# Prompt and sample tokens transposed once, unnormalized; their norm applied behind and between the value projections, in a written order

## The chip, the cores and the metric

The kernel runs on one core of a Trainium2 chip. The metric is the device time of one execution in microseconds (us). A NeuronCore has engines that run side by side, each through its own instructions in order: PE (TensorE, matmuls and transposes; PEld is its loading of weights), DVE (VectorE), ACT (ScalarE), POOL (GpSimd) and SP (SyncE, which here issues most DMAs). They meet through semaphores. Matmuls accumulate in PSUM and DVE or ACT empty it.

## The reference

One step of a two-layer decoder over 1104 tokens: 64 sample tokens (8 requests of 8), 16 meta tokens and 1024 prompt tokens. What the change touches is the beginning of the first layer, an mLSTM mixer on normalized tokens:

```python
def rmsnorm(x, g):
    xf = x.astype(jnp.float32)
    r = lax.rsqrt(jnp.mean(xf * xf, axis=-1, keepdims=True) + EPS)
    return (xf * r * g.astype(jnp.float32)).astype(x.dtype)

def mlstm_mixer(xn, C0, n0, m0, lead, w_in, b_ig, b_fg, mh_g, w_out):
    p = xn @ w_in
    ...
    q = heads(p[..., :HK], DK_A) * DK_A ** -0.5
    k = heads(p[..., HK:2 * HK], DK_A)
    v = heads(p[..., 2 * HK:2 * HK + HV], DV_A)
    og = p[..., 2 * HK + HV:2 * HK + 2 * HV]
    gi = p[..., 2 * HK + 2 * HV:2 * HK + 2 * HV + H_A]
    gf = p[..., 2 * HK + 2 * HV + H_A:]
    ...

def run_trunk(h, C0, n0, m0, lead, attend, prm):
    ...
            a, (C, n, m) = mlstm_mixer(rmsnorm(h, prm['norm_a'][i]), C0[i], n0[i], m0[i], lead, ...)
            h = h + a
```

Here HK is 512, HV is 1024 and the model width is 1024. A SwiGLU follows, then an attention layer on a paged cache with forget values, and a second SwiGLU. `r` is the root of the title (one number per token), `g` the gain (one number per feature).

## The kernel before

All is fp32. Each product is made of three matmuls of fp32r: an operand x is split into a high half xh (a cast, on ACT) and a low half xl = x - xh (on DVE), and `mm3` (lines 191 to 195) adds xh by high weights, xh by low weights and xl by high weights. Halves of weights are called whi and wlo, raw ones wraw.

The 1104 tokens are nine tiles: tile 0 with 80 tokens (samples and meta), tiles 1 to 8 with 128. The 1024 features are eight blocks of 128.

`load_x` (line 628) brings one tile after another into `xin` by DMA from SP, makes the sum of squares and the root on ACT (L644, L645), its reciprocal (L646) and the normalized `xn` on DVE (L647). It transposes `xn` on PE (tile xps, L655) and splits it into xh and xl (L267, L268), which stay in SBUF for all projections. It also transposes the raw `xin` (tile hps, L661), copies that into `hs` (L662, one half on DVE and one on ACT) and writes it to `hD` in DRAM (L663, DMA from POOL), the residual stream that the rest of the kernel reads back.

`phase_a` then makes the values in four groups of 256 columns, c in (3, 0, 1, 2) (line 92), through `tm_proj` (line 306): nine tiles each, 24 matmuls per tile into a PSUM tile `tmps`, of which there are four; `evac` copies them into `vA` on ACT (L695). Group 3 carries 16 gate columns more (L697). Next come `cache_prep` (line 807: 32 small DMAs of cached log-forget values through a page table, four transposes, a running sum on DVE, L829, eight DMAs to `csE`), three of the eight column blocks of `w_out_a` halved and written to DRAM (`wo_out`), and the q and k projections (`qk_out`, PSUM tile mmA). The gates are prepared next to them (`rec_prep`), then the gate projections and the recurrence follow.

Up to `qk_out` the order on each engine is set by the scheduler, from what is ready; PE's first rows below show how it mixes both transposes with group 3.

Of the kernel before, what the change touches and what calls it, by code (L numbers as in the profile page):

```python
# [93 lines left out]
class TwoNorms:  # L94
# [11 lines left out]
    def low(self, o, y, h):  # L106
        self.sub(o, y, h.bitcast(F32))
# [69 lines left out]
class Net:  # L177
# [19 lines left out]
    def consts(self):  # L197
# [15 lines left out]
        with self.pool("g0") as gp, self.pool("g0p", space=PSUM) as pp:  # L213
            rows = gp.tile([NG, P], F32, name="grows")
            for at, src, n in (
                (G_A, I["norm_a"][0], 8), (G_F, I["norm_ffn"].rearrange("l d -> (l d)"), 16),
                (G_KV, I["norm_kv"], 8), (G_B, I["norm_b"][0], 8), (G_FIN, I["norm_final"], 8),
                (G_MH, I["mh_norm_a"][0].rearrange("h d -> (h d)"), 8),
            ):
                nc.scalar.dma_start(rows[at : at + n, :], src.rearrange("(k p) -> k p", p=P))  # L220
            ps = pp.tile([P, NG], F32, name="gps")
            nc.tensor.transpose(ps, rows, self.ident[:NG, :NG])
            nc.vector.tensor_copy(self.gain, ps)
# [395 lines left out]
def _add(cls):  # L619
    def deco(f):  # L620
        setattr(cls, f.__name__, f)
        return f

    return deco


@_add(Net)
def load_x(self):

    nc, I = self.nc, self.I  # L630
    with self.pool("lx", bufs=2) as lp, self.pool("lxp", bufs=2, space=PSUM) as pp:
        gr = lp.tile([P, D], F32, name="gr", bufs=1)
        nc.scalar.dma_start(gr, I["norm_a"][0].partition_broadcast(P))
        for i, (t0, t1) in enumerate(TT):
            n = t1 - t0
            xin = lp.tile([P, D], F32, name="xin", bufs=3)
            if i == 0:
                nc.sync.dma_start(xin[:NS], I["x_sample"].rearrange("b t d -> (b t) d"))
                nc.sync.dma_start(xin[NS:T0], I["meta_tokens"])
            else:  # L640
                nc.sync.dma_start(xin, I["x_prompt"][0, (i - 1) * P : i * P, :])
            xn = lp.tile([P, D], F32, name="xn")
            r = lp.tile([P, 2], F32, name="r0")
            nc.scalar.activation(xn[:n], xin[:n], AF.Square, accum_out=r[:n, 0:1])  # L644
            nc.scalar.activation(r[:n, 1:2], r[:n, 0:1], AF.Sqrt, scale=1.0 / D, bias=self.eps[:n])  # L645
            nc.vector.reciprocal(r[:n, 1:2], r[:n, 1:2])  # L646
            nc.vector.scalar_tensor_tensor(out=xn[:n], in0=xin[:n], scalar=r[:n, 1:2], in1=gr[:n], op0=ALU.mult,  # L647
                                           op1=ALU.mult)
            hs = lp.tile([P, KT, P], F32, name="hs")
            for g in range(2):  # L650
                ks = slice(4 * g, 4 * g + 4)
                ps = pp.tile([P, 4, P], F32, name=self.uid("xps"), tag="xps")
                for k in range(4):
                    f = 4 * g + k
                    nc.tensor.transpose(ps[:, k, :n], xn[:n, f * P : (f + 1) * P], self.ident[:n, :n])  # L655
                xh, xl = self.xs
                self.split(ps[:, :, :n], xh[:, ks, t0:t1], xl[:, ks, t0:t1])
                ps = pp.tile([P, 4, P], F32, name=self.uid("hps"), tag="hps")
                for k in range(4):
                    f = 4 * g + k  # L660
                    nc.tensor.transpose(ps[:, k, :n], xin[:n, f * P : (f + 1) * P], self.ident[:n, :n])  # L661
                (nc.scalar.copy if g else nc.vector.tensor_copy)(hs[:, ks, :n], ps[:, :, :n])  # L662
            nc.gpsimd.dma_start(self.hD[:, :, t0:t1], hs[:, :, :n])  # L663


@_add(Net)
def phase_a(self, vt):
# [5 lines left out]
    with ExitStack() as c3:  # L673
# [14 lines left out]
        with ExitStack() as cw, self.pool("ppA0", bufs=4, space=PSUM) as pp:  # L688
            self.wpools(cw, 3, 4)
            self.load_x()  # L690
            for c in (3, 0, 1, 2):
                c0 = 2 * HA * DK + 256 * c

                def evac(i, m, ps):
                    nc.scalar.copy(v(i)[:m, 2 * c : 2 * c + 2, :DV], ps[:m, :256].rearrange("p (h d) -> p h d", h=2))  # L695
                    if c == 3:
                        nc.scalar.copy(gates[:m, i, :], ps[:m, 256:272])  # L697

                self.tm_proj([w_in[:, c0 : c0 + 256]] + ([w_in[:, 3072:3088]] if c == 3 else []), None, pp, "mm0", 4,
                             evac)  # L700
                if c == 3:
                    for n, out in ((NQ, self.q8), (NM, self.m16)):
                        self.row_mask(kp.tile([P, P // n, n], F32, name=self.uid("rm"), tag="rm"), out, n)

        pp = c3.enter_context(self.pool("ppA", bufs=2, space=PSUM))

        self.wpools(c3, 2, 3, side="left")
        self.cache_prep()


        self.woD = []

        def wo_out():
            m = len(self.woD)
            d = self.dram.tile([P, 2, KT, P], F32, name=f"woD{m}")
            for z, y in enumerate(self.load_w([I["w_out_a"][0][:, m * P : (m + 1) * P]])):
                nc.gpsimd.dma_start(d[:, z], y.bitcast(F32))
            self.woD.append(d)
# [88 lines left out]
def cache_prep(self):  # L807
# [5 lines left out]
    with self.pool("cp") as sp, self.pool("cpp", space=PSUM) as pp:  # L813
        lp = sp.tile([P, NPG, NB, HB], F32, name="lp")
        for b in range(NB):
            for n in range(NPG):
                j = b * NPG + n
                v = nc.sync.value_load(self.ptab[0:1, j : j + 1], min_val=0, max_val=I["cache_k"].shape[0] - 1)
                self.pages.append(v)
                nc.sync.dma_start(lp[:, n, b, :], I["cache_logf"][bass.DynSlice(v, 1)].rearrange("a p h -> (a p) h"))  # L820
        cs = sp.tile([P, PAST], F32, name="cs")
        lt = sp.tile([P, PAST], F32, name="csl")
        on = sp.tile([P, PAST], F32, name="cso")
        ps = pp.tile([P, 512], F32, name="csps")
        for n in range(NPG):
            nc.tensor.transpose(ps[:, n * P : n * P + P], lp[:, n].rearrange("p b h -> p (b h)"), self.ident)
        nc.scalar.activation(lt, ps, AF.Copy, scale=-1.0)
        nc.gpsimd.memset(on, 1.0)
        nc.vector.tensor_tensor_scan(cs, on, lt, 0.0, ALU.mult, ALU.add)  # L829
        nc.vector.tensor_copy(self.clast, cs[:, PAST - 1 : PAST])  # L830
        for q in range(NQ):
            nc.gpsimd.dma_start(self.csE.rearrange("b (h q) k -> q b h k", q=NQ)[q].rearrange("b h k -> (b h) k"), cs)
# [2012 lines left out]
```

## Time and profile before

| | |
|---|---|
| three runs, median (lowest to highest) | 2835.35 us (2833.57 to 2840.07) |
| the profiled execution | 2837.3 us |
| its span, first to last instruction | 2835.5 us, 60526 instructions |
| mean granted clock of PE | 0.996 |
| DMA | 469.45 MB, mean 166 GB/s |

The profile belongs to one execution, so times taken from it are set against 2837.3 us, not the median. Busy time of an engine is no bound by itself: a group of rows names the line, the engine, the operation, output and inputs by tile, how many, then busy us and mean ns, then the idle time before them and what ended it. Matmuls overlap in the array, so what a matmul costs is read from the distance of starts, not from its length.

### The profile page before, as it was taken

Reading aid. Unit: us, or ns where it says so; the run is one execution under the profiler, and the core shown is the slowest. Engines: PE = TensorE matmul, PEld = TensorE weight load, DVE = VectorE, ACT = ScalarE, POOL = GpSimd, SP = SyncE. Lnnn points to the kernel's source line nnn. Section 1 sums busy time; section 2 is a strip of 40 time slices with the busy share of each in tenths; the row PEclk is TensorE's granted clock in tenths of the full one; section 3 lists DMA queues with packets and bytes.
Section 4 is the critical chain, followed back from the end, with each engine's and each line's share of the span. In section 5 each row is a group of like instructions: output and inputs, shape, how many; then the busy total and the mean of one; then the engine's idle time right before and its main releaser. Section 6 shows DMA issues by size and latency. Waiting matters only on the chain. (4 is left out here: it accounts for less than half of the span.)

```text
span 2835.5 us, 60526 instructions
## 1 busy us (share of the span) xinstructions
PE 2769.2 (98%) x23614; PEld 2656.7 (94%) x23614; DVE 1772.6 (63%) x3921; ACT 1167.3 (41%) x2279; POOL 831.1 (29%) x1307
## 2 busy tenths in 40 slices
PE   7999999999999999999999999999999999999998
PEld 7999889999999999999999888677999999999998
DVE  5142566888887666573455443777478888765656
ACT  5232363433233234443444444877443323323345
POOL 3022234132233222124353202454312322323111
PEclk9999999999999999999999999999999999999999
DMA  6365538245555365544453686342524565527556
GB/s 195 111 201 140 139 111 284 76 135 175 175 165 161 106 228 180 199 147 153 151 181 126 226 297 225 129 168 88 157 76 135 169 176 168 161 90 231 181 194 214
DMA packets 428393, 469.45 MB, mean 166 GB/s; under 512 B 40030, under 2 KB 354522, under 8 KB 427082
## 3 DMA queue, kind: packets, MB, share of 16 engines
q1 hardware_dynamic: 378978, 316.78, 36.0%
q0 software_dynamic: 43600, 143.14, 15.3%
q10 hardware_dynamic: 5528, 5.65, 0.6%
q8 instruction: 186, 3.05, 0.4%
q14 instruction: 101, 0.83, 0.1%
HBM read 318.25 MB, written 147.21 MB: 164 GB/s over the span
## 5 line engine op out<-in xcount | busy, mean ns | idle before, releaser
L1416 PE MATMUL m<-xh,slot 128*128 128x276 f32 x2752 | 540.6, 290 | 1.8 <-ACT fs L1445 1.8
L1416 PEld LDWEIGHTS m<-xh,slot 128*128 128x128 f32 x2752 | 439.6, 188 | 3.8 <-ACT fs L1445 2.2
L1416 PE MATMUL m<-xl,slot 128*128 128x276 f32 x1376 | 397.1, 289 | 0.0
L1416 PEld LDWEIGHTS m<-xl,slot 128*128 128x128 f32 x1376 | 258.6, 188 | 0.0
L193 PE MATMUL tmps<-slot,xh 128*128 128x256 f32 (+2 forms) x864 | 243.4, 282 | 0.0
L195 PE MATMUL tmps<-slot,xl 128*128 128x256 f32 (+2 forms) x864 | 240.9, 279 | 0.0
L194 PE MATMUL tmps<-slot,xh 128*128 128x256 f32 (+2 forms) x864 | 240.9, 279 | 0.0
L268 DVE TENSOR_TENSOR slot<-slot,slot 128x1024 fp32r<-128x1024 f32 x124 | 162.8, 1314 | 60.5 <-ACT slot L267 59.0
L267 ACT CAST slot<-slot 128x1024 fp32r<-128x1024 f32 x124 | 129.6, 1046 | 143.6 <-PE m L1416 109.8
L194 PEld LDWEIGHTS tmps<-slot,xh 128*128 128x128 f32 (+1 forms) x864 | 159.3, 184 | 0.1
L195 PEld LDWEIGHTS tmps<-slot,xl 128*128 128x128 f32 (+1 forms) x864 | 158.7, 184 | 0.0
L193 PEld LDWEIGHTS tmps<-slot,xh 128*128 128x128 f32 (+1 forms) x864 | 158.4, 183 | 0.2
L193 PE MATMUL mmA<-xh,whi 128*128 128x384 f32 (+1 forms) x384 | 134.4, 350 | 0.1
L195 PE MATMUL mmA<-xh,wlo 128*128 128x384 f32 (+1 forms) x384 | 127.2, 331 | 0.0
L194 PE MATMUL mmA<-xl,whi 128*128 128x384 f32 (+1 forms) x384 | 127.2, 331 | 0.0
L268 DVE TENSOR_TENSOR slot<-vA,slot 128x1024 fp32r<-128x1024 f32 (+1 forms) x59 | 82.3, 1397 | 32.7 <-ACT slot L267 31.5
L268 DVE TENSOR_TENSOR slot<-Ht,slot 128x1024 fp32r<-128x1024 f32 (+1 forms) x59 | 82.0, 1393 | 32.8 <-ACT slot L267 31.6
L256 DVE TENSOR_TENSOR wlo<-wraw,whi 128x1024 fp32r<-128x1024 f32 (+1 forms) x32 | 39.0, 1226 | 100.9 <-ACT whi L255 76.5
L267 ACT CAST slot<-Ht 128x1024 fp32r<-128x1024 f32 (+1 forms) x59 | 60.9, 1037 | 95.5 <-PE m L1416 88.5
L267 ACT CAST slot<-vA 128x1024 fp32r<-128x1024 f32 (+1 forms) x59 | 60.8, 1035 | 95.5 <-PE m L1416 86.6
L1520 DVE TENSOR_TENSOR ws<-ws 128x128 f32<-128x128 f32 x264 | 93.8, 355 | 8.9
L2667 ACT ACTIVATE s<-s,nb 128x272 f32<-128x272 f32 (+7 forms) x126 | 98.8, 786 | 0.0
(788 smaller groups left out, 8677.7 us busy)
## 6 DMA issues: line engine op xcount, KB each, us to landing
ws<-in_w_down SPq DMA_DIRECT2D x176, 128.0 KB, 2.5
sD<-ws SPq DMA_DIRECT2D x176, 128.0 KB, 2.2
slot<-sD SPq DMA_DIRECT2D x40, 512.0 KB, 5.5
slot<-in_w_gate_up SPq DMA_DIRECT2D x36, 512.0 KB, 4.5
kp<-in_cache_k SPq DMA_DIRECT2D x32, 512.0 KB, 6.2
vp<-in_cache_v SPq DMA_DIRECT2D x32, 512.0 KB, 6.5
vA<-in_w_gate_up SPq DMA_DIRECT2D x26, 512.0 KB, 4.8
Ht<-in_w_gate_up SPq DMA_DIRECT2D x26, 512.0 KB, 4.3
```

The lines of the kernel that those rows point to most:

```text
L193: mm(ps, sh, mh, start=first, stop=False)
L194: mm(ps, sh, ml, start=False, stop=False)
L195: mm(ps, sl, mh, start=False, stop=last)
L256: low = lambda: nc.vector.tensor_tensor(out=lo, in0=raw, in1=hi.bitcast(F32), op=ALU.subtract)
L267: self.nc.scalar.copy(hi, src)
L268: self.nc.vector.tensor_tensor(out=lo, in0=src, in1=hi.bitcast(F32), op=ALU.subtract)
L1416: nc.tensor.matmul(u.ps[h, b], w[p][:, k], x[q][:, k], start=first and k == i == 0, stop=k == 3 and i == 2, skip_group_check=True)
L1520: tt(out=o, in0=a, in1=b, op=ALU.subtract)
L2667: nc.scalar.activation(ss[z, u], ss[z, u], AF.Exp, bias=nb[:, z : z + 1], accum_out=sm[:, u, z : z + 1])
```

## The change

Tokens are transposed once, raw. The transposed raw tile is split into xh and xl, and copied to `hs` for `hD`. Groups 0, 3 and 1 (now in this order, group 3 two tiles behind group 0) run on the raw halves: the gain is multiplied into the weights as they are halved, feature block by feature block, and the root into the values as ACT copies them out of PSUM. The sums of squares go into `ss`, the roots into `rr`, their reciprocals to `rD` in DRAM.

During groups 1 and 2 the raw tiles are read back from `hD` into one of three buffers `hr`, with the roots spread over partitions (`rb`), multiplied by gain and root (`norm`), and split anew into xh and xl (`high`, `low`), each tile once group 1 has passed it. Group 2, q, k and the gates use these normalized halves. `cache_prep`, three blocks of `w_out_a` and the first block of q weights (`q0`) are worked in between; 48 of the 56 rows of gains are loaded later and by POOL. In this whole stretch the order on PE, SP, DVE and ACT is the one in which the code is written (`manual_schedule`); POOL is left to the scheduler.

```diff
         with self.pool("g0") as gp, self.pool("g0p", space=PSUM) as pp:
...
+            rows = gp.tile([8, P], F32, name="grows")
+            nc.scalar.dma_start(rows, I["norm_a"][0].rearrange("(k p) -> k p", p=P))
+            nc.scalar.activation(c.tile([P, 1], F32, name="root"), self.eps, AF.Sqrt)
...
-def load_x(self):
+def values_a(self, v, kp, gates, w_in, c3):
...
+        self.wpools(cw, 2, 4)
+        xr = cw.enter_context(self.pool("xr", bufs=3, side="right"))
+        cw.enter_context(self.tc.manual_schedule(engines={E.PE, E.SP, E.DVE, E.Activation}))
...
+        def halve(c, z):
...
+            if c == 2:
+                self.split(raw, hi, lo)
+                return
+            for k in range(4):
+                y = hi[:, k, :256]
+                nc.scalar.activation(y, raw[:, k], AF.Copy, scale=G(4 * z + k))
+                nc.vector.scalar_tensor_tensor(out=lo[:, k, :256], in0=raw[:, k], scalar=G(4 * z + k),
+                                               in1=y.bitcast(F32), op0=ALU.mult, op1=ALU.subtract)
+            if c == 3:
+                self.split(gw[:, 4 * z : 4 * z + 4], hi[:, :, 256:], lo[:, :, 256:])
...
+            def out():
+                r = 1.0 if c == 2 else rr[:m, i : i + 1]
+                nc.scalar.activation(v(i)[:m, 2 * c : 2 * c + 2, :DV],
+                                     ps[:m, :256].rearrange("p (h d) -> p h d", h=2), AF.Copy, scale=r)
...
+        def reload(i):
...
+            nc.sync.dma_start(y[:, :, :n], self.hD[:, :, t0:t1])
+            nc.sync.dma_start(rb, rD[i].partition_broadcast(P))
+
+        def norm(i):
...
+            for k in range(KT):
+                nc.vector.scalar_tensor_tensor(out=y[:, k, :n], in0=y[:, k, :n], scalar=G(k), in1=rb[:, :n],
+                                               op0=ALU.mult, op1=ALU.mult)
...
+        turn(0)
+        halves(0)
+        halve(0, 0)
+        turn(1)
+        keep(0)
+        halve(0, 1)
+        squares(0)
+        halves(1)
+        keep(1)
+        for i in range(NT + 2):
+            if i < NT:
+                out = values(0, i)
...
+            if i + 2 < NT:
+                turn(i + 2)
+            if i == 0:
+                squares(1)
+            if i < NT:
+                nc.vector.reciprocal(rr[: size(i), i : i + 1], rr[: size(i), i : i + 1])
+                out()
+            if i + 4 < NT:
+                load(i + 4)
+            if i + 2 < NT:
+                halves(i + 2)
+                keep(i + 2)
+                squares(i + 2)
+            if i < 2:
+                fetch(3, i)
+                halve(3, i)
...
+            if i >= 2:
+                values(3, i - 2)()
+
+        for i in range(3):
+            reload(i)
+        fetch(2, 0)
+        fetch(2, 1)
+        def R(i):
+            def job():
+                norm(i)
+                high(i)
+
+                def rest():
+                    low(i)
+                    if i + 3 < NT:
+                        reload(i + 3)
+                return rest
+            return job
...
+        jobs = {0: lambda: self.cache_prep(*cache, tp, "xps"), 1: R(0), 2: R(1), 3: opened,
+                4: R(2), 5: R(3), 6: lambda: halve(2, 1), 7: R(4), 8: R(5), 9: lambda: more(2), 10: R(6), 11: R(7),
+                12: lambda: more(w_in[:, :P]), 13: R(8), 14: self.wo_split, 16: self.wo_split}
+        after = None
+        for j in range(2 * NT):
+            values(1 + j // NT, j % NT)()
+            rest = jobs[j]() if j in jobs else None
+            if after:
+                after()
+            after = rest
...
-        for m in range(3):
-            wo_out()
...
-                wh, wl = self.load_w([w_in[:, m * P : (m + 1) * P]])
+                wh, wl = self.load_w([w_in[:, m * P : (m + 1) * P]]) if m else self.q0
```

`turn` transposes a tile, `halves` splits it, `keep` copies it for `hD`, `squares` makes sum and root, `fetch` loads half a group's weights.

PE at the very start, before (rows of one engine in its order; hps is the raw transpose, xps the normalized one, tmps a tile of values):

```order
L222 MATMUL gps<-ident,grows 128x56
L661 MATMUL hps_160<-ident,xin 128x80 x4
L661 MATMUL hps_173<-ident,xin 128x80 x4
L661 MATMUL hps_196<-ident,xin 128x128 x4
L661 MATMUL hps_209<-ident,xin 128x128 x3
L655 MATMUL xps_153<-ident,xn 128x80 x4
L655 MATMUL xps_166<-ident,xn 128x80 x4
L661 MATMUL hps_209<-ident,xin 128x128
L661 MATMUL hps_232<-ident,xin 128x128 x4
L193 MATMUL tmps_484<-whi_471,xh 80x272
```

and now:

```order
L218 MATMUL gps<-ident,grows 128x8
L731 MATMUL xps_163<-ident,xin_148 128x80 x4
L731 MATMUL xps_168<-ident,xin_148 128x80 x4
L731 MATMUL xps_187<-ident,xin_153 128x128 x4
L731 MATMUL xps_192<-ident,xin_153 128x128 x4
L193 MATMUL tmps_221<-whi_177,xh 80x256
```

Two tiles are turned once, then the first values of group 0 begin; the scheduler had turned tiles 0 and 1 twice and part of tile 2 before its first value matmul of group 3.

DVE from the last weights of the raw groups to the running sum of the cache, before:

```order
L256 TENSOR_TENSOR wlo_1147<-wraw_1145,whi_1146 128x1024
L887 TENSOR_TENSOR gates<-gates,gbias 128x144
L256 TENSOR_TENSOR wlo_1153<-wraw_1151,whi_1152 128x1024
L889 TENSOR_SCALAR gates<-gates 128x144
L256 TENSOR_TENSOR wlo_1999<-wraw_1997,whi_1998 128x1024
```

and now (hr is a reloaded tile, rb its spread roots):

```order
L1016 SCALAR_TENSOR_TENSOR cp_566<-cp_567 128x512
L1017 COPY clast<-cp_566 128x1
L700 SCALAR_TENSOR_TENSOR hr_1246<-hr_1246,gain,rb_1247 128x80 x8
L700 SCALAR_TENSOR_TENSOR hr_1250<-hr_1250,gain,rb_1251 128x128 x8
L708 TENSOR_TENSOR xl<-hr_1246,xh 128x8x80
L272 TENSOR_TENSOR wlo_1407<-wraw_1258,whi_1406 128x1024
L708 TENSOR_TENSOR xl<-hr_1250,xh 128x8x128
L700 SCALAR_TENSOR_TENSOR hr_1254<-hr_1254,gain,rb_1255 128x128 x8
```

Where DVE had only low halves of weights and two gate operations, the running sum of the cache now comes first and the nine normalizations with their low halves follow, two tiles and one piece of weights in turn.

SP's DMAs behind the cache loads, now:

```order
L693 DMA hr_1254<-hD 128x8x128
L694 DMA rb_1255<-rD 128x128
L654 DMA wraw_1258<-in_w_in_a 128x4x256
L654 DMA wraw_1260<-in_w_in_a 128x4x256
L693 DMA hr_1376<-hD 128x8x128
L694 DMA rb_1377<-rD 128x128
L851 DMA wraw_1415<-in_w_out_a 128x8x128
L851 DMA wraw_1417<-in_w_out_a 128x8x128
```

and what stood at the same place before:

```order
L252 DMA wraw_1997<-in_w_out_a 128x8x128
L252 DMA wraw_2006<-in_w_out_a 128x8x128
L252 DMA wraw_2015<-in_w_out_a 128x8x128
L252 DMA wraw_2150<-in_w_in_a 128x8x128
L252 DMA wraw_2255<-in_w_in_a 128x8x128
```

The reloads of hD and the roots stand in SP's queue between the weights of group 2 and those of `w_out_a`.

More of the change, by code (lines that the diff above doesn't have):

```diff
@@ L650, in load_x, with turn, halves @@
+        def turn(i):
+            n = size(i)
+            for g in range(2):
+                ps = xps[i, g] = tp.tile([P, 4, P], F32, name=self.uid("xps"), tag="xps")
+                for k in range(4):
+                    f = 4 * g + k
+                    nc.tensor.transpose(ps[:, k, :n], xin[i][:n, f * P : (f + 1) * P], self.ident[:n, :n])
+        def halves(i):
+            n, (t0, t1) = size(i), TT[i]
             for g in range(2):
                 ks = slice(4 * g, 4 * g + 4)
-                ps = pp.tile([P, 4, P], F32, name=self.uid("xps"), tag="xps")
@@ L653, in load_x @@
[L653 to L661, printed above, removed]
```

219 lines of the change are left out of this document (150 added, 69 removed).

## Prediction

> **What bounds the kernel now.** I read busy times and slices on the page first, then PE's waits (us in total, times, longest) over the stretch that the change rewrites and behind it, then busy time by stretch (busy us of PE, PEld, DVE, ACT, POOL; granted clock, DMA share, GB/s), then the timeline.
>
> ```profile
> PE 2769.2 (98%) x23614; PEld 2656.7 (94%) x23614; DVE 1772.6 (63%) x3921; ACT 1167.3 (41%) x2279; POOL 831.1 (29%) x1307
> PE   7999999999999999999999999999999999999998
> L193 PEld LDWEIGHTS mmA<-xh,whi x45: 187/188/190, 145.1 to 169.8; 128*128 128x128 f32 x45
> PE sp L2640 <- DVE mx L2644: 7.1, 16, 0.9
> ```
>
> PE (TensorE) is busy 98% of the span and its only weak slice is the first (71 us). The rewritten stretch ends where the q/k matmuls into tile mmA begin, at 145.1 us. Behind that, PE's largest group of waits is 7.1 us in 16 pieces, and nothing there hangs on a clock time. So I take whatever mmA's start gains as gained at the end, and the question is when mmA starts.
>
> ```profile
> PE gps L222 <- POOL rm L2273: 5.3, 1, 5.3
> PE hps L661 <- ACT hs L662: 5.4, 3, 2.1
> PE hps L661 <- DMA xin<-in_x_prompt: 3.9, 3, 2.8
> PE tmps L193 <- ACT vA L695: 3.9, 2, 2.2
> 5.30:16.10 10.80, 5.58 (x29) 4.50 (x30) 4.70 (x10) 7.47 (x13) 10.61 (x56) 1.00 0.84 232
> 16.10:50.00 33.90, 29.50 (x219) 28.05 (x218) 26.37 (x40) 24.77 (x54) 10.45 (x20) 0.95 0.88 286
> 51.49 1.07 PE L655 MATMUL xps<-ident,xn 128*128 128x128 f32 x8
> 52.32 0.37 PE L193 MATMUL tmps<-whi,xh 128*128 128x272 f32 x1
> 58.65 0.37 ACT L695 COPY vA<-tmps 128x256 f32<-128x256 f32 x1 [2.58 <-PE tmps L195]
> 61.68 0.37 ACT L695 COPY vA<-tmps 128x256 f32<-128x256 f32 x1 [2.58 <-PE tmps L195]
> 123.19 0.37 ACT L695 COPY vA<-tmps 80x256 f32<-80x256 f32 x1 [2.36 <-PE tmps L195]
> 142.23 0.38 ACT L695 COPY vA<-tmps 128x256 f32<-128x256 f32 x1 [2.35 <-PE tmps L195]
> 22.00:24.00 2.00, 2.00 (x11) 2.00 (x10) 0.98 (x2) 1.83 (x4) 0.86 (x1) 0.50 1.09 349
> 24.00:26.00 2.00, 2.00 (x14) 2.00 (x13) 0.61 (x2) 0.60 (x2) 0.00 (x0) 0.69 1.00 324
> 100.00:104.00 4.00, 4.00 (x23) 4.00 (x22) 3.50 (x3) 3.16 (x7) 0.00 (x0) 0.57 0.68 191
> ```
>
> Here are the unit prices. Where PE streams, ACT empties one tile of values per 61.68 - 58.65 = 3.03 us with 272 columns, and per (142.23 - 123.19)/7 = 2.72 us with 256. Eight transposes (one tile, turned once) take 52.32 - 51.49 = 0.83 us. So the 145.1 us hold 9 x 3.03 + 27 x 2.72 = 100.7 us of value matmuls and 18 x 0.83 = 14.9 us of transposes. The granted clock fell twice, after PE had stood still: (0.50 + 0.31) x 2 = 1.6 us lost from 22 to 26, and 0.43 x 4 = 1.7 us from 100 to 104. The remaining 26 us are standing still: the first 5.3, the waits above, and the paced start between 5.3 and 50, where a matmul's modelled length hides part of the gaps.
>
> **The change, part by part.** *Transposes*: 72 of 144 go, 9 x 0.83 = 7.5 us off PE. *Root and gain*: the root moves into the scale of the copy that empties PSUM, which exists already (0.37 us), and the gain into the halving of the weights, as four operations of 256 columns each on ACT and DVE (VectorE) instead of one of 1024. *Start*: the fixed order has to be followed by hand up to where PE streams, with these rows.
>
> ```profile
> 8.00:12.00 4.00, 1.09 (x4) 0.71 (x4) 0.08 (x1) 2.38 (x3) 4.00 (x29) 1.00 0.97 329
> 4.94 1.28 ACT L644 ACT_TABLE_LOAD   x1 [4.94 <-DMA xin<-in_meta_tokens]
> 5.58 1.33 PE L661 MATMUL hps<-ident,xin 80*128 80x80 f32 x8
> L644 ACT ACTIVATE xn<-xin 128x1024 f32<-128x1024 f32 x8 | 8.6, 1072 | 2.2 <-DMA xin<-in_x_prompt 2.2
> L644 ACT ACTIVATION_READ_ACCUMULATOR xn<-xin 128x1 f32 x8 | 1.6, 201 | 0.0
> L645 ACT ACTIVATE r<-r,eps 128x1 f32<-128x1 f32 x8 | 2.4, 302 | 0.0
> L267 ACT CAST xh<-xps 128x512 fp32r<-128x512 f32 x16 | 9.0, 595 | 2.2 <-PE xps L655 1.9
> 102.14 0.64 ACT L695 COPY vA<-tmps 80x256 f32<-80x256 f32 x2
> L268 DVE TENSOR_TENSOR xl<-xps,xh 128x512 fp32r<-128x512 f32 x16 | 10.4, 686 | 3.1 <-ACT xh L267 3.0
> L662 DVE COPY hs<-hps 128x512 f32<-128x512 f32 x8 | 5.5, 682 | 4.3 <-DMA hD<-hs 3.5 <-PE hps L661 0.8
> L401 DVE SCALAR_TENSOR_TENSOR vA<-vA,gain,sq 128x276 f32<-128x276 f32 x8 | 3.6, 496 | 0.0
> ```
>
> Tile 0 is there at 4.94 as before, and SP's next pieces of 512 KB come 1.6 us apart at 329 GB/s: weights (0,0) at 6.5, tile 1 at 8.1, weights (0,1) at 9.7, tile 2 at 11.3, tile 3 at 13.2. From 9.7 us ACT has work without a break, and I let it end the start. The halving of weights (0,1) is four operations at some 0.3 us (two of 256 columns took 0.64), until 10.9. Squares and root of tile 0 are 1.07 + 0.20 + 0.30 = 1.6, until 12.5. Then xh of tile 1 (1.2), squares of tile 1 (1.6), first evacuation (0.4), xh of tile 2 (1.2), squares (1.6), weights (3,0) with the gate columns (1.4), evacuation (0.4), xh of tile 3 (1.2), squares (1.6), weights (3,1) (1.4): 12.0 us, until 24.5. DVE's low halves of those follow: four of 256 columns, just under the 0.50 us of 276 columns each, so up to 2.0 us less what overlaps; 26.5 us. By then PE has done three tiles of group 0 and the first of group 3 and turned tiles 0 to 4; it stands still some 4 us before the second half of that first group-3 tile. Below: 22, if DVE keeps up and PE is never held by more than ACT. Above: 33, if DVE, with (0.69 + 0.68) x 2 + 2.0 = 4.7 us a tile beside ACT's 4.8, hands its wait on to ACT at each root.
>
> *Stream*: left are 8 x 3.03 + 6 x 2.72 + 18 x 2.72 = 89.5 us of values, 4 x 0.83 = 3.3 of turns and 0.5 for the five transposes of gains and cache sums: 93.3 us. From there ACT's 3.7 us and DVE's 2.9 us of work in a step of 5.75 to 6.6 us leave PE first. *Clock*: the stand-still at 22 to 26 costs one dip, 1.7 us; none is the lower end, two (3.3) the upper.
>
> Beside the sum stands a rule. The Trainium skill, "TensorE: Matmul & The Clock Gate", Part 1, says that the array drops to half clock after an idle window of about 3.4 us and comes back after as long a busy one; by it each new gap of this order costs 1.7 us more than itself, and the trace agrees (0.50 at 22 us, 0.57 at 100). By that rule a late gap of 5 us in the next part would make the sum 6.7 instead of 5.
>
> *Normalizing in place*: new work on DVE, eight operations of 128x128 and one low half a tile, between groups 1 and 2 (third and fourth), fed by a reload of 512 KB per tile through three buffers.
>
> ```profile
> L1137 DVE SCALAR_TENSOR_TENSOR eb<-eb,tmA,cap x65: 291/342/1567, 229.7 to 406.1; 128x128 f32<-128x128 f32 x64, 80x80 f32<-80x80 f32 x1
> 298.05 0.61 DVE L1301 SCALAR_TENSOR_TENSOR C<-C,wcS,cs 128x129 f32<-128x129 f32 x2 [0.42 <-PE cs L1300]
> L256 DVE TENSOR_TENSOR wlo<-wraw,whi 128x1024 fp32r<-128x1024 f32 x30 | 36.4, 1222 | 100.9 <-ACT whi L255 76.5 <-DMA woD<-wlo 17.8 <-issue 6.5
> L829 DVE TENSOR_TENSOR_SCAN cs<-cso,csl 128x512 f32<-128x512 f32 x1 | 1.2, 1224 | 42.5 <-ACT csl L827 42.5
> qk<-qkD POOLq DMA_DIRECT2D x8, 512.0 KB, 4.6
> wraw<-in_w_in_a SPq DMA_DIRECT2D x9, 512.0 KB, 10.0
> DMA to landing us min/median/max: 2.0/5.5/8.3
> ```
>
> Two neighbours of 129 columns took 0.61 us, so eight take 0.61 x 4 = 2.4 us; one by one, at 0.34, 2.7. With sums above, group 1 begins at 26.5 + 1.7 + 24.2 + 16.3 + 3.4 = 72.1. DVE's cache scan waits for its first tile and ACT, and ends at 77. Up to the low half of tile 8 DVE then has 9 x 2.4 + 9 x 1.2 + 5 x 1.2 (weights) = 38.4 us, so tile 8 is ready at 115.4, against 72.1 + 0.4 + 17 x 2.72 = 118.7 when PE wants it. At 2.7 it would be 118.1. Slack is 0.6 to 3.3 us. Behind each low half SP reloads the tile three further on; the q/k read of equal size landed in 4.6 us, the residual hD (last row) in up to 8.3, and from a tile's low half to the next use of its buffer DVE has some 5 us of other work for every second tile. A landing of 4.6 costs nothing, one of 8.3 about 3 us at three places, 9 us less the slack. I take 1.5 us for PE; 0 and 8 are the ends. What is queued behind a late tile is ACT's cast for it and the next evacuations; PE has four PSUM tiles, 8 us, before it notices. Weights for the first q/k group are now fetched and halved ahead (last of DVE's fixed rows, about 117), which the stream hides.
>
> **Sum.** 26.5 + 1.7 + 93.3 + 1.5 = 123.0 us for mmA's start, against 145.1: 22 us less. The profiled execution took 2837.3 us; 2837.3 - 22.1 = 2815.2. The median shown is 2835.35, 1.95 lower, so 2813.3, say 2813.5.
>
> **Rivals.** (a) *The start stays paced*: 33 us, two dips, and a late gap of 1.5 give 33 + 3.3 + 93.3 + 1.5 = 131.1, a gain of 14, 2821.4. For it: PE's 5.4 us behind ACT in the old start, and DMA at 0.97 share. Against it: ACT loses a second drain of each transpose and DVE the 1.3 us scaling. (b) *The start flows*: 22, no dip, no late gap, 115.3, a gain of 30, 2805.6. Against it: ACT's chain of fixed rows. (c) *The reload ring decides*: tiles 2, 5 and 8 share a buffer, so tile 8 waits for two reloads in turn. To end over 0.2% slower than before, PE must lose 22 + 5.7 us; with 3 us slack and 5 us covered per turn, each reload would have to land in 5 + 31/2 = 20 us. The slowest comparable row is 10.0 us for weights. Then it ends near 2842. (d) *The gain is not handed on*: the q/k, gate and recurrence stretch has its own bound and PE waits there by as much more, 2835. Against it: the 98%.
>
> **How the numbers follow.** My forecast, with a gain of 18 to 26, has 0.52; (a) 0.26, (b) 0.12, (c) 0.05, (d) 0.05. A measurement of this kernel tells about 0.2% (5.7 us) from no change. Forecast, (a) and (b) are all faster by more: 0.90; same 0.05, slower 0.05. The range runs from (b)'s 2806 to somewhat past (a), where the paced start (33 and two dips) meets a late loss of 6: 33 + 3.3 + 93.3 + 6 = 135.6, a gain of 9.5, 2826.
>
> **What would show it.** ACT's last piece of weights (3,1) near 24.5 us and a gap on PE before it confirm the start; group 1 beginning at 72 confirms the stream; low half of tile 8 before 118 and no PE wait on it clears the ring; mmA's first matmul at 123 and PE's waits behind it as before carry the gain to the end. A start of mmA past 131, or PE waits behind it grown by over 5 us, would make me wrong.

## The result and the profile after

The changed kernel is slower by 0.2%: 2842.26 us median of 17 runs (2838.58 to 2849.61) against 2835.70 of 17 runs of the kernel before (2832.89 to 2843.21); ratio 1.0021, 95% interval 1.0014 to 1.0029. The forecast was 2813.5. The profiled execution took 2838.96 us, span 2837.3, and is one of the fastest of its kernel.

From the page of the changed kernel, busy times and PE's slices:

```profile
PE 2771.8 (98%) x23543; PEld 2661.9 (94%) x23543; DVE 1797.4 (63%) x4025; ACT 1178.2 (42%) x2299; POOL 833.3 (29%) x1313
PE   8999999999999999999999999999999999999998
```

The first slice rose from 7 to 8 tenths. PE has 71 instructions fewer (23543 against 23614) and is still busy 2.6 us longer. So some instructions seem to take longer; where, the windows below show.

Next the first loads of mmA's operands (count, shortest/median/longest ns, first to last start):

```profile
L193 PEld LDWEIGHTS mmA<-xh,whi x68: 186/188/190, 138.0 to 174.5; 128*128 128x128 f32 x68
```

And PE's waits (us in total, times, longest):

```profile
PE sp L2827 <- DVE mx L2831: 6.9, 15, 0.8
PE tmps L195 <- DVE xl L708: 3.4, 2, 3.1
PE tmps L193 <- ACT whi L271: 3.1, 2, 2.6
```

mmA starts at 138.0 us instead of 145.1: 7.1 us earlier, not 22. Behind it, the largest wait of PE is as it was (6.9 us; 7.1 before). But the span is longer by 2837.3 - 2835.5 = 1.8 us, so 8.9 us were lost behind mmA, and only 1.1 of them by standing still (PE is idle there for 39.6 us, 38.5 before). The windows of two stretches behind show how (us, PE busy (count), granted clock, DMA share, GB/s). Here is the kernel before:

```profile
680.00:920.00 240.00, 240.00 (x1891) 1.00 0.57 169
1340.00:1540.00 200.00, 200.00 (x1750) 1.00 0.46 156
```

And the changed kernel:

```profile
680.00:920.00 240.00, 240.00 (x1884) 1.00 0.57 168
1340.00:1540.00 200.00, 200.00 (x1719) 1.00 0.47 153
```

PE is busy throughout in all four rows, at the full granted clock, and does less: 0.4% fewer matmuls in the up and gate projections (680 to 920) and 1.8% fewer in the projections of the second layer (1340 to 1540, tile tmps, with some 100 short transposes among them). PE's instructions and their order are the same there in both kernels. The whole second stage says the same. Here are its matmuls of line 193 (shortest/median/longest ns, first to last start), first before, then now:

```profile
L193 PE MATMUL tmps<-slot,xh x864: 275/276/488, 1259.1 to 1577.4; 128*128 128x256 f32 x141, 128*80 128x256 f32 x18, 128*128 128x272 f32 x13, 128*80 128x272 f32 x1
L193 PE MATMUL tmps<-slot,xh x864: 277/280/485, 1256.6 to 1580.2; 128*128 128x256 f32 x141, 128*80 128x256 f32 x18, 128*128 128x272 f32 x13, 128*80 128x272 f32 x1
```

The stage took 318.3 us and now takes 323.6.

In the head the trouble is on ACT, DVE and SP. First the changed kernel's start (timeline: start, us, operation, and in brackets the idle time ahead and what ended it):

```profile
9.12 1.71 ACT L666 ACTIVATE whi<-wraw,gain 128x256 fp32r<-128x256 f32 x4 [1.60 <-DMA wraw<-in_w_in_a]
11.84 1.71 ACT L666 ACTIVATE whi<-wraw,gain 128x256 fp32r<-128x256 f32 x4 [1.01 <-DMA wraw<-in_w_in_a]
23.60 0.48 ACT L682 ACTIVATE vA<-tmps,rr 128x256 f32<-128x256 f32 x1 [0.80 <-DVE rr L780]
28.13 0.23 ACT L271 CAST whi<-gw 128x64 fp32r<-128x64 f32 x1
77.83 0.28 PE L193 MATMUL tmps<-whi,xh 128*80 128x256 f32 x1
```

Its windows there (busy us of PE, PEld, DVE, ACT, POOL; granted clock, DMA share, GB/s):

```profile
25.00:30.00 5.00, 2.38 (x13) 1.81 (x12) 3.94 (x10) 4.18 (x12) 0.86 (x1) 0.78 0.98 324
30.00:32.00 2.00, 2.00 (x11) 2.00 (x10) 1.98 (x4) 1.97 (x5) 0.00 (x0) 0.50 0.53 162
32.00:34.00 2.00, 2.00 (x11) 2.00 (x11) 0.58 (x2) 0.38 (x2) 0.85 (x1) 0.50 0.72 188
34.00:36.00 2.00, 2.00 (x17) 2.00 (x16) 0.00 (x0) 0.08 (x1) 0.00 (x0) 0.85 0.99 310
```

The weights are there at 9.1 and 11.8 us (predicted 6.5 and 9.7), each halving is 1.71 us long, ACT's copy out of PSUM waits for DVE's reciprocal, and weights (3,1) are ready on ACT at 28.4 us instead of 24.5. PE stands still for 2.6 us, and the granted clock is low up to past 34 us: 0.22 x 5 + 0.50 x 4 + 0.15 x 2 = 3.4 us of it are lost. Group 1 begins at 77.8 us (last row of the timeline). Now the timeline of SP, POOL and DVE around it:

```profile
65.83 14.58 SPq L1003 DMA_DIRECT2D cp<-in_cache_logf  x12
80.51 0.62 SPq L693 DMA_DIRECT2D hr<-hD  x1
85.88 1.27 SPq L654 DMA_DIRECT2D wraw<-in_w_in_a  x2
84.39 4.32 POOL L1019 DMA_DIRECT2D csE<-cp  x8 [22.17 <-DVE cp L1016]
82.86 1.23 DVE L1016 TENSOR_TENSOR_SCAN cp<-cp 128x512 f32<-128x512 f32 x1 [2.28 <-ACT cp L1014]
84.91 1.79 DVE L700 SCALAR_TENSOR_TENSOR hr<-hr,gain,rb 128x80 f32<-128x80 f32 x8 [0.64 <-DMA rb<-rD]
98.04 1.23 DVE L272 TENSOR_TENSOR wlo<-wraw,whi 128x1024 fp32r<-128x1024 f32 x1 [7.48 <-ACT whi L271]
100.31 4.28 DVE L700 SCALAR_TENSOR_TENSOR hr<-hr,gain,rb 128x128 f32<-128x128 f32 x16
109.30 4.29 DVE L700 SCALAR_TENSOR_TENSOR hr<-hr,gain,rb 128x128 f32<-128x128 f32 x16
132.89 1.22 DVE L708 TENSOR_TENSOR xl<-hr,xh 128x1024 fp32r<-128x1024 f32 x1
```

And two windows of it:

```profile
84.00:97.00 13.00, 13.00 (x111) 13.00 (x110) 4.95 (x19) 3.15 (x6) 4.32 (x8) 1.00 1.04 343
130.00:140.00 10.00, 6.41 (x38) 6.13 (x38) 4.77 (x5) 4.66 (x8) 3.96 (x26) 0.83 0.85 270
```

SP needs 14.58/12 = 1.2 us for each small cache load, so the first reload leaves at 80.5 us and the weights of group 2 at 85.9. Then eight writes to csE (256 KB each, 2 MB) start at 84.4, and from 84 to 97 us the DMA engines are full (share 1.04). The weights arrive late and DVE stands still for 7.48 us. Its first normalization, at 84.9, waits only 0.64 us for the reload: ahead of it in the written order stands the running sum, which ends at 84.1. From then on DVE goes round once in 109.30 - 100.31 = 9.0 us (two tiles and one piece of weights); tile 8's low half is done at 134.1, and PE waits 3.1 us for it. The granted clock falls once more there (0.83 from 130 to 140, 1.7 us lost).

### The profile page after: what moved, and what is told of

Its sections match the earlier page's. It is cut to its first block, busy times and chain, and to the rows that moved or that the text cites. A ratio compares the mean times of both kernels' runs of the same rounds, so it can differ in the third digit from the quotient of the medians.

```text
span 2837.3 us, 60545 instructions
## 1 busy us (share of the span) xinstructions
PE 2771.8 (98%) x23543; PEld 2661.9 (94%) x23543; DVE 1797.4 (63%) x4025; ACT 1178.2 (42%) x2299; POOL 833.3 (29%) x1313
## 5 line engine op out<-in xcount | busy, mean ns | idle before, releaser
L2287 DVE TENSOR_REDUCE ss<-sqb 128x4 f32<-128x256 f32 (+1 forms) x72 | 30.2, 419 | 104.3 <-ACT sqb L2286 103.4
```

Source lines behind the costliest of these rows:

```text
L2287: nc.vector.tensor_reduce(out=ss[:m, i, :], in_=sq[:m].rearrange("p (h d) -> p h d", d=DH), op=ALU.add, axis=AX.X)
```

## The experiments

Two questions were put: what makes matmuls slower behind mmA, and why mmA starts at 138 and not at 123. The new constant tile `root` (one column, 32 bytes of each partition) stands ahead of xh and xl, and moves them and all later tiles on the left side of SBUF by 32 bytes: xh from byte 6176 to 6208. The first theory blames that shift. In the table, mmA's start is that of its first matmul (145.1 in the kernel before, 138.1 in the changed one), and L2 is the time from the first to the last start of line 193 into tmps in the second layer (318.3 and 323.6).

| run | what it is | mmA starts, us | L2, us | median, us | ratio to before, 95% |
|---|---|---|---|---|---|
| e1_root_in_mask | changed, shift undone | 139.7 | 317.3 | 2831.97 | 0.9982 (0.9972 to 0.9992) |
| e2_root_64 | changed, shift 64 bytes | 138.3 | 326.8 | 2840.11 | 1.0010 (1.0001 to 1.0020) |
| e3_before_pad | before, shift 32 | 145.1 | 323.5 | 2850.12 | 1.0048 (1.0034 to 1.0061) |
| e8_before_pad_behind_x | before, shift 32 behind xl only | 143.2 | 317.4 | 2836.61 | 0.9999 (0.9990 to 1.0008) |
| e14_before_pad_96 | before, shift 96 | 144.5 | 328.9 | 2851.89 | 1.0050 (1.0037 to 1.0063) |
| e4_fetch_first | changed, other order on SP | 137.5 | 323.5 | 2842.87 | 1.0020 (1.0011 to 1.0029) |
| e5_batch | changed, register loads first | 141.4 | 323.5 | 2841.25, one run | - |
| e6_early_cache | e5, running sum early | 144.6 | 323.5 | 2849.97 | 1.0041 (1.0027 to 1.0055) |
| e7_all | e6 + e4 + e1 | 148.8 | 317.3 | 2841.15 | 1.0013 (1.0004 to 1.0022) |
| e9_spread_loads | e7, register loads spread | 137.7 | 318.2 | 2831.11 | 0.9973 (0.9964 to 0.9981) |
| e10_root_ahead | e9, reciprocal a step ahead | 134.7 | 318.2 | 2833.16 | 0.9981 (0.9972 to 0.9989) |
| e11_flood_in_group | e10, running sum back in group 1 | 130.8 | 318.2 | 2827.32, one run | - |
| e13_flood_again | e11 again | 132.3 | 317.4 | 2826.83 | 0.9958 (0.9945 to 0.9971) |
| e12_loads_one_step_on | e11, loads a step later | 127.4 | 318.2 | 2825.39 | 0.9954 (0.9938 to 0.9970) |

### The place of xh and xl

**The shift undone.**

```diff
-            nc.scalar.activation(c.tile([P, 1], F32, name="root"), self.eps, AF.Sqrt)
+            nc.scalar.activation(rm[:, NQ + NM : NQ + NM + 1], self.eps, AF.Sqrt)
```

> The changed kernel, but the root of eps that only loads ACT's table is written into a free column of rowm instead of a tile of its own, so xh, xl, vA and what follows lie at the addresses that they have in the kernel before (xh at byte 6176 of a partition instead of 6208). Address theory: the drift behind mmA goes (the value stage of layer 2 at 1290 to 1580 us takes 113.5 ns a matmul as before, not 116), mmA still starts at 137 to 138 us, so the time is about 7 us below the kernel before: 2828 to 2831. Rival (the drift belongs to the chip, or to what DMAs do beside the stream): 2840 to 2844 as the changed kernel, 116 ns a matmul.

**Another shift.**

```diff
-            nc.scalar.activation(c.tile([P, 1], F32, name="root"), self.eps, AF.Sqrt)
+            nc.scalar.activation(c.tile([P, 16], F32, name="root")[:, :1], self.eps, AF.Sqrt)
```

> The changed kernel with the tile root of 64 bytes instead of 32, so that all later tiles lie 64 bytes further on than in the kernel before (xh at 6240). If it is the place within 64 bytes that counts: as with no shift, 2828 to 2831 and 113.5 ns a matmul in the value stage of layer 2. If any shift, or a place within 128 bytes or more, counts: 116 ns and 2840 to 2844, or worse.

**The shift alone, in the kernel before** (and 96 bytes, with `[P, 24]`, in e14_before_pad_96).

```diff
         self.q8, self.m16 = rm[:, :NQ], rm[:, NQ : NQ + NM]
+        nc.vector.memset(c.tile([P, 1], F32, name="root"), 1.0)
```

> The kernel before with a tile of one column (32 bytes) put behind rowm and nothing else, so that xh lies at 6208. Address theory: mmA starts where it did (144 to 147 us), the stream behind it is 9 to 13 us slower: 2845 to 2849, ratio 1.003 to 1.005. Rival: no change, 2834 to 2838.

**The shift behind xh and xl**, in the kernel before:

```diff
             self.xs = [xp.tile([P, KT, PX + T], F32R, name=f"x{s}")[:, :, PX:] for s in "hl"]
+            self.nc.vector.memset(xp.tile([P, 1], F32, name="root"), 1.0)
```

> The kernel before with the 32 bytes put behind xh and xl instead of ahead of them: xh and xl stay at 6176 and 43040, vA, Ht and all later tiles move by 32 bytes. If it is the place of xh and xl that sets the pace of the stream: 2834 to 2838 and 113.5 ns a matmul in the value stage of layer 2. If it is that of the other tiles: 2846 to 2851 as with the tile ahead of them.

> The kernel before with 96 bytes ahead of xh and xl, so that xh lies at 6272. If the place within 64 bytes sets the pace of the up and gate projections (32 bytes further on cost 0.4% there, 64 bytes nothing): as with 32, so 2845 to 2852, with the value stage of layer 2 at 116 ns a matmul. If every shift has a pace of its own: something else, 2836 to 2860.

The same two windows, first the changed kernel with the shift undone, then the kernel before with the shift alone:

```profile
680.00:920.00 240.00, 239.98 (x1890) 1.00 0.56 167
1340.00:1540.00 200.00, 200.00 (x1759) 1.00 0.45 152
```

```profile
680.00:920.00 240.00, 240.00 (x1884) 1.00 0.56 166
1340.00:1540.00 200.00, 199.94 (x1717) 1.00 0.47 152
```

The pace goes with the shift and not with the change. Both expectations came out but for sizes: with the shift undone mmA starts 1.7 us later and the median lies 1 us higher than I had put, and e3's median lies 1 us above its range. The one-column tile alone makes the kernel before 0.48% slower (13.7 us by the medians of that call), and taking it out of the changed kernel brings 1.0021 down to 0.9982. The address theory holds: the rival fell in both runs. With the shift undone the changed kernel also keeps most of what mmA gained: 5.4 us there, 4.4 us by the medians.

With the tile behind xl, where vA, Ht and the rest of the left side move and xh and xl do not, nothing changes:

```profile
1340.00:1540.00 200.00, 199.84 (x1750) 1.00 0.48 156
```

So it is the place of xh and xl; the matmuls that slow down read only these and the weights, and the tiles of the weights, on the right side, did not move. The expectation that places repeat every 64 bytes fell. First 64 bytes further on (changed kernel), then 96 (before):

```profile
680.00:920.00 240.00, 240.00 (x1891) 1.00 0.56 167
1340.00:1540.00 200.00, 200.00 (x1701) 1.00 0.46 150
```

```profile
680.00:920.00 240.00, 240.00 (x1891) 1.00 0.57 169
1340.00:1540.00 200.00, 199.99 (x1685) 1.00 0.47 152
```

Divided out, an operation of PE in the second stretch takes 200/1750 = 114.3 ns at no shift, 116.3 at 32 bytes, 117.6 at 64 and 118.7 at 96, and the whole stage 318.3, 323.5, 326.8 and 328.9 us: it gets worse step by step. The up and gate projections lose 0.4% at 32 bytes and nothing at 64 or 96. Why is open: no run tells whether the distance to the streamed weights, which stayed where they were, or the place itself counts. The medians lose more (13.7 us in e3) than the profiled executions (2844.5 - 2835.5 = 9.0 of span). The profiled one is the fastest of e3's five, and the clock differs: in the kernel before it fell to half five times for 3.4 us (at 22, 100, 192, 1592 and 1752 us, 8.6 us lost in all), in e3 once for 6.8 us (at 191, 3.4 us lost). With that set aside the matmuls lose 9.0 + 5.2 = 14.2 us, by this estimate, which agrees with the medians.

### The start of mmA

**The order on SP.**

```diff
+        fetch(2, 0)
+        fetch(2, 1)
         for i in range(3):
             reload(i)
-        fetch(2, 0)
-        fetch(2, 1)
```

> The changed kernel with the two weight loads of group 2 issued by SP ahead of the three reloads instead of behind them. Theory (SP's order): they land before the eight writes to csE fill the DMA engines, DVE's 7.5 us of standing still before the low half of weights (2,0) goes, its chain of normalizing ends near 128 us instead of 135.5, mmA starts at 130 to 132 instead of 138, and the time falls by 6 to 8 us to 2834 to 2836. Rival (the DMA engines are full from 84 to 100 us whatever the order): the reloads land later by what the weights gain, mmA starts at 136 to 138, time 2840 to 2842.

DVE's timeline in this run:

```profile
88.98 1.79 DVE L700 SCALAR_TENSOR_TENSOR hr<-hr,gain,rb 128x80 f32<-128x80 f32 x8 [4.36 <-DMA rb<-rD]
93.03 2.19 DVE L700 SCALAR_TENSOR_TENSOR hr<-hr,gain,rb 128x128 f32<-128x128 f32 x8 [2.25 <-DMA rb<-rD]
97.64 1.23 DVE L272 TENSOR_TENSOR wlo<-wraw,whi 128x1024 fp32r<-128x1024 f32 x1 [1.69 <-ACT whi L271]
```

The 7.5 us went from the weights to the reloads (4.36 + 2.25), and the low half of the weights starts at 97.6 as before. The rival was right, but for a median 0.9 us above its range: with full DMA engines, order among SP's loads moves the wait and does not shorten it.

**SP's register loads ahead of all cache loads, then the running sum early, then all together.**

```diff
             v = nc.sync.value_load(self.ptab[0:1, j : j + 1], min_val=0, max_val=I["cache_k"].shape[0] - 1)
             self.pages.append(v)
+    for b_ in range(NB):
+        for n in range(NPG):
+            v = self.pages[b_ * NPG + n]
             nc.sync.dma_start(lp[:, n, b_, :], I["cache_logf"][bass.DynSlice(v, 1)].rearrange("a p h -> (a p) h"))
```

> The changed kernel with SP's 32 register loads of the page table ahead of the 32 small cache loads, not one before each. SP theory (1.26 us a load in turn delays the reloads): the cache loads end near 60 us instead of 80, the reloads go out when the roots have landed in rD (74 us), and mmA starts at 130 to 132 us instead of 138. Rival (the writes to csE fill the DMA engines after the running sum, whatever SP did before): the loads end near 60 us too, but the weights of group 2 still land at 95 us or later and mmA starts at 136 to 138.

```diff
+            if i == NT:
+                self.cache_prep(*cache, tp, "xps")
...
-        jobs = {0: lambda: self.cache_prep(*cache, tp, "xps"), 1: R(0), 2: R(1), 3: opened,
+        jobs = {1: R(0), 2: R(1), 3: opened,
```

> As the last one, and the four transposes and the running sum of the cache one place earlier in the written order than rD's users need the DMA engines: behind the first tile loop's ninth step instead of in group 1. Theory (the csE writes, 2 MB, fill the DMA engines just when reloads and weights are wanted): these writes now run at 66 to 73 us, the weights of group 2 land by 88 us, DVE's wait of 7.5 us for them goes, mmA starts at 129 to 132 us, the time falls by 6 to 8 us to 2834 to 2836 (later tiles still lie 32 bytes further on). Rival (DVE's own chain of normalizing, 8.9 us for two tiles and a weight, is the bound and starts no earlier): mmA at 135 or later, 2839 to 2842.

> The last one with the weight loads of group 2 ahead of the reloads, and the root in a free column of rowm, so that later tiles lie where the kernel before has them. If both theories hold they add up: mmA starts at 127 to 131 us, no drift behind it, 2820 to 2826, 10 to 16 us below the kernel before. If the gain of the head is lost again before the recurrence ends (PE loses 2.4 us there in the changed kernel): 2826 to 2832.

All three were misses. From the last of them, SP's row of the cache loads in the timeline:

```profile
59.72 23.74 SPq L1008 DMA_DIRECT2D cp<-in_cache_logf  x32
```

And PE's wait for them:

```profile
PE csps L1018 <- DMA cp<-in_cache_logf: 12.3, 2, 12.0
```

The loads through a register cost 23.74/32 = 0.74 us each even after all register loads are done, and these had already held SP up to 59.7 us. Issuing them in another order saves nothing; the cache loads still end at 83 us, and with the transposes moved ahead PE itself waits 12 us for them. The end "near 60 us" that I expected left the register loads no time of their own. That e7_all, with mmA at 148.8, is still 8.8 us faster than e6_early_cache, with mmA at 144.6, fits the shift, which e7_all undoes.

**The register loads spread**, over e7_all:

```diff
         load(2)
+        self.pages = []
+        nc.sync.dma_start(self.ptab, I["page_table"].rearrange("b n -> (b n)").unsqueeze(0))
...
+            if i < 4:
+                self.page_loads(8)
```

> As the run with everything put together, but the page table is fetched at the start and SP's 32 register loads of it are spread, eight at a time, over the first four steps of the first tile loop, where SP waits for tokens anyway. Theory: a register load costs SP 0.6 us and a cache load 0.7 us whatever their order, so only an earlier start helps: cache loads end at 56 to 60 us, PE waits less than 1 us for them, csE is written at 68 to 75 us, the first normalizing begins at 78 to 82 us instead of 84.9 and has no wait of over 2 us for weights or reloads, mmA starts at 126 to 131 us, 2822 to 2828. If the loads between the tokens' loads hold tokens up, the start is later by that and the time is 2828 to 2834.

**The reciprocal a step ahead**, over that:

```diff
-                nc.vector.reciprocal(rr[: size(i), i : i + 1], rr[: size(i), i : i + 1])
                 out()
...
                 squares(i + 2)
+            if i + 1 < NT:
+                root(i + 1)
             if i < 2:
                 fetch(3, i)
```

`root(i)` is that reciprocal; `root(0)` stands ahead of the first evacuation.

> The last one with DVE's reciprocal of a tile's root issued one step earlier, ahead of the low halves of weights (3,0) and (3,1), so that ACT's copy out of PSUM does not wait for it (0.7 to 1.0 us a step in the changed kernel's start). Theory (the start is a ping-pong between ACT and DVE): a step of the start takes 4.6 to 4.9 us instead of 5.4, PE's stand-still at 25 to 30 us shrinks from 2.6 us by 1 us or more, mmA starts 2 to 4 us earlier than in the last one. Rival (the start is held by landings and by ACT's own work): no change within 1 us.

**The running sum back in group 1**, over e10_root_ahead (the diff of e6_early_cache undone), and the same kernel timed:

> The last one, but the transposes and the running sum of the cache stay where the changed kernel has them, in group 1, so csE is written at 82 to 95 us, beside the reloads. Theory (the 2 MB of csE fill the DMA engines): reloads issued after 82 us land in 8 us or more, DVE's waits for reloads and weights come back (5 us or more in all up to 100 us), mmA starts 3 to 7 us later than in the last one. Rival (only SP's late start mattered): mmA within 1 us of the last one.

> The run with the running sum left in group 1 once more, timed: mmA at 130 to 131.5 us; if the one look was no accident 2826 to 2830, ratio 0.996 to 0.998. The order 'reloads, then csE' then beats 'csE, then reloads' by 3 to 5 us; if this is no cause, the time is that of the latter, 2832 to 2834.

Spreading (eight register loads in each of the first four steps) took mmA from 148.8 to 137.7 us, short of the 126 to 131 expected; the time, 2831.11, lies where I had put it if these loads hold up those of tokens. With the reciprocal ahead mmA starts at 134.7, 3.0 us earlier, where 2 to 4 were expected. But PE's stand-still at 25 to 30 us did not shrink, though the theory asked for it: ACT no longer waits for the reciprocal of tile 1, and then waits 2.98 us for weights (3,1). The running sum ends only 1.5 us earlier (74.9 against 76.4), and the rest came later. The medians do not show the 3.0 us; the profiled execution of e10 lost 3.4 us of clock from 1805 to 1825 us (0.83 there, 1.00 in e9). The third result came out on the wrong side for my theory: with csE written later, mmA starts 3.9 us earlier. The timelines of SP, POOL and DVE show why. First csE early (e10_root_ahead):

```profile
77.25 1.00 SPq L693 DMA_DIRECT2D hr<-hD  x1
75.23 4.29 POOL L1035 DMA_DIRECT2D csE<-cp  x8 [12.38 <-DVE clast L1033]
87.41 1.79 DVE L700 SCALAR_TENSOR_TENSOR hr<-hr,gain,rb 128x80 f32<-128x80 f32 x8 [5.84 <-DMA rb<-rD]
```

Then csE late (e11_flood_in_group):

```profile
76.26 0.62 SPq L693 DMA_DIRECT2D hr<-hD  x1
84.46 4.29 POOL L1033 DMA_DIRECT2D csE<-cp  x8 [21.08 <-DVE cp L1030]
84.26 3.89 DVE L700 SCALAR_TENSOR_TENSOR hr<-hr,gain,rb 128x80 f32<-128x80 f32 x16
```

SP comes to the first reload at 76 to 77 us in both. Writing csE at 75 us puts its 2 MB right in front of it; writing it at 84 us leaves the first reloads a free way, and DVE does 16 normalizing operations with no wait. So the two do collide, as supposed, but the cure is to let the reloads out ahead of it, not csE ahead of the reloads. The timed run confirms it, 0.9958 against 0.9981, though mmA starts at 132.3 this time, 0.8 us past what I had put: DVE's chain began at 84.3 again, but the clock was 0.91 from 120 to 140 us and 1.00 in e11.

**The register loads one step later**, over e11_flood_in_group:

```diff
-            if i < 4:
+            if 0 < i < 5:
                 self.page_loads(8)
```

(These lines also move up, ahead of the block `if i == 4` that issues the cache loads.)

> The run with the running sum left in group 1, but SP's four lots of eight register loads begin one step later, behind the load of weights (3,1) and not ahead of it. Theory (in that run PE's longest wait, 4.7 us for the gate columns of weights (3,0), comes from SP's register loads ahead of the weights' loads): this wait falls to 2 us or less, mmA starts at 127 to 129.5 us instead of 130.8, 2823 to 2827. Rival (the wait is ACT's own queue, and what the start gains is lost again to DVE's chain of normalizing): mmA at 130 to 131.5, 2826 to 2830.

PE's wait for weights of group 3 (its second half, (3,1), by ACT's timeline, not (3,0)), first in e11_flood_in_group and then in this run:

```profile
PE tmps L193 <- ACT whi L271: 4.7, 1, 4.7
```

```profile
PE tmps L193 <- ACT whi L271: 1.1, 1, 1.1
```

And this run's windows around the old stand-still:

```profile
25.00:30.00 5.00, 3.50 (x27) 1.00 0.92 307
30.00:35.00 5.00, 5.00 (x46) 1.00 0.58 215
```

The wait falls from 4.7 to 1.1 us, as the theory asked, and the clock no longer drops there. mmA starts at 127.4 and the kernel takes 2825.39 us, 0.46% below the kernel before: the only version besides e13_flood_again that is faster by clearly more than 0.2%. The 1.4 us between the medians of these two are within their spread, so mmA's earlier start is shown and a gain in time over e13_flood_again is not.

## Why the prediction was wrong

**Two steps failed, and they add up.** The forecast was 2813.5. mmA gained 7.1 us where 22.1 were put, 15.0 less. Behind mmA the stream lost (2842.26 - 2835.70) + 7.1 = 13.7 us by the medians where nothing was put. 2813.5 + 15.0 + 13.7 = 2842.2, against 2842.26 measured. That this closes is no check, since the 13.7 is what the medians leave; by the profiled executions it is 8.9, with 1.7 us less clock lost behind mmA than before (3.4 against 5.1). The check is e3: the tile alone costs 13.7 us.

**"Whatever mmA's start gains I take as gained at the end"** failed. It was argued from waits, and the waits did behave: PE's 7.1 us in 16 pieces became 6.9 in 15. What I named as the sign that it fails, PE's waits behind mmA grown by over 5 us, did not come either; the same matmuls ran slower at the full clock. Rival (d), the gain not handed on (2835), named this step, with another cause. The row of the diff that did it is the one that makes the tile `root`: I costed what it computes, not where it puts everything after it. Shown by e1, e3 and e8. With xh and xl in their old place the step is better, but not whole: of mmA's gain the medians keep 4.4 of 5.4 us in e1, 7.5 of 7.4 in e9, 5.4 of 10.4 in e10 and 12.1 of 17.7 in e12. Some of what is missing is clock lost far behind the start, as in e10; the rest was not traced. Here the Trainium skill, "SBUF — State Buffer", section "Operand start alignment", allows any address that is a multiple of the element's size and says that this "is about legality, not speed"; all places tried here are legal, and they differ by 0.5% in time.

**The sum for mmA's start, 123.0, was 15 us short.** By its terms:

- *Start 26.5.* ACT's last piece came at 28.4, not 24.5: landings were 2.1 to 2.6 us later than the pieces of 1.6 us apart gave, four halving operations took 1.71 us and not 1.2, and ACT waited 0.7 to 1.0 us per step for the reciprocal, which I had not put in its chain. e10 took the last of these out for tile 1, and mmA started 3.0 us earlier, 1.5 of which the running sum shows.
- *One clock dip, 1.7.* Right in kind, wrong in size: PE stood still at 25 to 30 us, and the low clock there cost 3.4 us, as much as the two dips (3.3) of the upper end; the dip at the wait for tile 8 cost 1.7 more. By the rule that the prediction quotes from the Trainium skill, "TensorE: Matmul & The Clock Gate", Part 1, a gap of this order costs 1.7, an estimate; the first one here cost twice that.
- *Group 1 begins at 72.1.* Its first matmul was at 77.8, 5.7 us late; 3.9 of these are ACT's chain above, and the clock dip, 1.7 longer than put, is about the rest.
- *DVE: 38.4 us without a break from 77, tile 8 at 115.4.* The unit price held (2.19 us for eight operations, 2.4 put). The chain began at 84.9 and not at 77, since the running sum ahead of it ended at 84.1: group 1 was 5.7 us late, and the sum came 6.3 us behind its start where 4.9 were put. 84.9 + 38.4 = 123.3; up to 134.1 DVE stood still for 14.4 us, 7.5 for weights behind csE's writes, 6.0 for ACT's casts (1.2 to 2.3 in each round) and 0.9 for a reload, and its work took 34.8 us, 3.6 less than put. I had put 1.5 us for all lateness; 0 and 8 were the ends, and from group 1 to mmA it took 138.0 - 77.8 = 60.2 us where 123.0 - 72.1 = 50.9 were put, 9.3 us more. The start of mmA past 131, named as a sign of being wrong, is here.
- *What was left out.* SP's 32 cache loads in written order, 40 us long, and csE's 2 MB at that place. I gave a cost to each reload and none to what is queued ahead of them on SP and on the DMA engines.

**The rivals.** (a), the paced start, was half true, 5.7 us of its 8. (c), the reload ring, gave 2842, which is the time measured, but that is luck: PE did wait at its place, tile 8's low half, yet DVE waited for no reload behind the first two (0.64 and 0.92 us), and no reload took 20 us. What it lost came from one collision of 13 us with other transfers, from ACT's casts and from the address. No single rival contained the address.

## What to carry to other kernels

A new tile, however small, moves all that is allocated behind it, and a stream of matmuls can change its pace for that alone (here by 1.6 to 3.3% in one stage and up to 0.5% of the kernel): put it where nothing moves, or run the old kernel with a dummy tile of that size to learn the price. In a fixed order, count what each queue issues ahead of a needed load, register loads included. And let a needed load out ahead of a bulk write; where the load cannot leave yet, hold the bulk write back.

## What the runs showed of the hardware

- The pace of matmuls, most of them of 256 columns, depended on the byte at which xh and xl lie: 114.3, 116.3, 117.6 and 118.7 ns from one operation of PE to the next with 0, 32, 64 and 96 bytes added, with no wait and at a granted clock of 1.00. Other tiles of the left side moved by 32 bytes cost nothing (0.9999, interval 0.9990 to 1.0008).
- A small load from an address in a register held SP for 0.74 us with the register long filled (e7_all; 32 in 19.72 us, 0.62 each, in e12_loads_one_step_on), and 1.2 us together with filling it.
- From 84 to 97 us the DMA engines moved 343 GB/s at a share of 1.04; the loads issued around then took the wait in either order: 7.48 us for weights, or 4.36 + 2.25 us for reloads (e4_fetch_first).
- After PE had stood still for 2.6 us, the granted clock was low up to past 34 us, and 3.4 us of it were lost (changed kernel, 25 to 36 us); after the waits before 26 and 104 us in the kernel before, 1.6 and 1.7 us were.
